# Down projection of a hybrid layer: the product P2 last, its resident blocks loaded ahead, the final norm by half rows

## The chip, the cores and the metric

The kernel runs on one core of one Trainium2 chip. The metric is the device time of that core in microseconds; smaller is better. Three runs of the kernel before took 1548.82, 1553.07 and 1555.38 us, so the median is 1553.07 us. One more execution was taken with the hardware profiler; all rows below come from it.

## What is computed

The kernel is one layer of a diffusion backbone: an adaLN-modulated norm, a token mixer with a gated DeltaNet and a Mamba-2 part, an output projection with a gated residual, then a gated MLP with a 3x3 convolution and a second gated residual, and a final RMSNorm. The change touches only what follows the MLP's gate, the down projection and the final norm. Of the reference:

```python
D_MODEL = 1024; SEQ = 1024; D_FF = 2816; EPS = 1e-6

def conv_glu(h, w_gate, w_up, conv_w, conv_b, w_down, on_grid):
    a = h @ w_gate
    ...
    return (jax.nn.silu(a) * (h @ w_up)) @ w_down

def rmsnorm(x, g):
    x32 = x.astype(jnp.float32)
    y = x32 * lax.rsqrt(jnp.mean(x32 * x32, axis=-1, keepdims=True) + EPS)
    return (y * g.astype(jnp.float32)).astype(x.dtype)

        x = x + g2 * conv_glu(modulate(rmsnorm(x, norm2_g[l]), sh2, sc2), *ffn_params, True)
    ...
    return rmsnorm(x, final_norm_g)
```

## The kernel before, in words

The down projection multiplies a 1024 x 2816 matrix by a 2816 x 1024 one. Both are cut into 2 x 2 parts and seven products P1 to P7 replace the usual eight (Strassen's method in Winograd's form): sums of parts go into a product, and sums of products give the four quarters of the result. The four quarters are tokens 0 to 511 or 512 to 1023 (row tiles t = 0 to 3 or 4 to 7 of 128 tokens each) by columns 0 to 511 (`LOH`) or 512 to 1023 (`HIH`). While the gate and up products run, `asums` and `wsums` write the sums of parts to DRAM (`sa_d`, `sw_d`).

Each product is a sum over 11 blocks (`NP`). `block` (L1407 and after) loads two tiles of 128 x 512 floats, 256 KB each, on the SP queue (L1418): `ra` from `sa_d`, the stationary side, and `rb` from `sw_d` or from `w_down`, the moving side. Each tile is split into a high part, a rounded copy that ACT makes (L1419, `sh` and `vh`), and a low part, a subtraction on DVE (recorded at the helper's line L95, `sl` and `vl`). `mul` (L1433) then makes three matmuls for each of four row tiles, so 12 in a block: high by high, and the two mixed ones. There are two buffers each for `ra` and `rb`, three each for `sh`, `sl`, `vh`, `vl`.

The eight PSUM banks form two sets of four, `accA` and `accB`. Products alternate between them, so a product's banks are read out ("evacuated") while the next product runs in the other set. The order is P1, P6, P2, P7, P5, P4, P3. The evacuation after each product keeps sums in `s1`, `s2`, `s3` (`sn` in the rows, 128 x 512 for each row tile) and, once a quarter is whole, `put` multiplies it by the gate row `g2row` into a temporary `tm` and adds that to the residual `x1[t]` (`x` in the rows): two DVE operations of 128 x 512.

The last product, P3, is treated apart. Its first three blocks (`HEAD`) run as the others do. For its last eight, the high and low parts go to eight places of their own in `mxh` and `mxl`, tiles that held the MLP's input before and are free by then; these are called resident blocks here. Then, for each row tile t, all matmuls of the eight resident blocks are to follow, then `put` and `final`.

`final(t, last)` is the norm of a whole row tile: ACT squares 128 x 1024 values and sums them along the row, DVE adds the epsilon, POOL raises the sum to the power -1/2 (L1289), DVE multiplies the row tile by that and by the gain row `gfrow` (one SCALAR_TENSOR_TENSOR, L107), and two DMAs write the halves, one from the SP queue and one from ACT's (L1573). For the last row tile it goes by halves (power at L1569). `final` runs for tiles 4 to 7 after P4, so beside P3, and for tiles 0 to 3 at the end.

The order on each engine is made when the kernel is built: a scheduler of the language places the instructions by its own estimate of their times, and each engine then runs its list strictly in order. A late instruction holds up all behind it on its engine.

Of the kernel before, what the change touches and what calls it, by code (L numbers as in the profile page):

```python
# [13 lines left out]
ALU = mybir.AluOpType  # L14
# [59 lines left out]
def hybrid_layer(ctx: ExitStack, tc: tile.TileContext, x, c, cx, c_ctx, w_ada, b_ada, norm1_g, w_in,  # L74
# [1325 lines left out]
    PRODS = ("P1", "P6", "P2", "P7", "P5", "P4", "P3")  # L1400
# [34 lines left out]
    def product(p, acc, js, first, last):  # L1435
        for j in js:
            ops = block(p, j, *parts())
            for t in range(4):
                mul(acc[t], t, ops, first and j == js[0], last and j == js[-1])

# [96 lines left out]
    with pool("p3") as p3:  # L1537
# [15 lines left out]
        def final(t, last):  # L1553
            if "f" not in rows:
                rows["f"] = T(p3, [P, D], "gfrow")
                nc.sync.dma_start(rows["f"], final_norm_g.partition_broadcast(P))
            jk = T(p3, [P, D], f"fj{t}", tag="fj", bufs=2)
            ot = T(p3, [P, D], f"ot{t}", tag="ot", bufs=3)
            halves = [slice(0, 512), slice(512, D)]
            if not last:  # L1560
                rs = rstd_tok(x1[t], jk, t, 1)
                stt(ot, x1[t], rs, rows["f"], ALU.mult, ALU.mult)
            else:
                rs, a = ss2[:, 1, t:t + 1], ss2[:, 0, 0:2]
                for c, q in enumerate(halves):
                    act(jk[:, q], x1[t][:, q], AF.Square, accum_out=a[:, c:c + 1])
                tt(rs, a[:, 0:1], a[:, 1:2], ALU.add)
                ts(rs, rs, 1.0 / D, ALU.mult, EPS, ALU.add)
                nc.gpsimd.tensor_tensor(rs, rs, mhalf[:, 0:1], op=ALU.pow)  # L1569
            for c, q in enumerate(halves):  # L1570
                if last:
                    stt(ot[:, q], x1[t][:, q], rs, rows["f"][:, q], ALU.mult, ALU.mult)
                (nc.scalar if c else nc.sync).dma_start(out[t * P:(t + 1) * P, q], ot[:, q])  # L1573

        allj = range(NP)
        product("P6", accB, range(NP - 1), True, False)
# [6 lines left out]
        product("P2", accA, allj, True, True)  # L1583
        for t in range(4):
            m = tmp_()
            tt(m, accA[t], s1[:, t, :], ALU.add)
            put(t, LOH, m)
        product("P7", accB, allj, True, True)
        for t in range(4):
            tt(s3[:, t, :], accB[t], s2[:, t, :], ALU.add)  # L1590
# [57 lines left out]
```

## Time and profile before

| what | value |
|---|---|
| median of three runs | 1553.07 us (1548.82 to 1555.38) |
| the profiled execution's own time | 1557.59 us |
| its span (first to last event of the core) | 1555.9 us |
| TensorE (PE) busy | 1454.9 us, 94% |
| VectorE (DVE) busy | 1093.4 us, 70% |
| ScalarE (ACT) busy | 695.1 us, 45% |
| GpSimd (POOL) busy | 514.8 us, 33% |
| matmuls of the seven products (L1433), part of the chain that ended last | 13% of the span |

The rows below are from the profiled execution, with times counted from the start of its span. The profiled time is 1.7 us longer than its span. "Idle before" in brackets is how long an engine stood still before an instruction, with what ended the wait. The granted clock (PEclk) is the share of TensorE's full clock that the chip allowed in a stretch.

### The profile page before, as it was taken

Reading aid. Unit: us, or ns where it says so; the run is one execution under the profiler, and the core shown is the slowest. Engines: PE = TensorE matmul, PEld = TensorE weight load, DVE = VectorE, ACT = ScalarE, POOL = GpSimd, SP = SyncE. Lnnn points to the kernel's source line nnn. Section 1 sums busy time; section 2 is a strip of 40 time slices with the busy share of each in tenths; the row PEclk is TensorE's granted clock in tenths of the full one; section 3 lists DMA queues with packets and bytes.
Section 4 is the critical chain, followed back from the end, with each engine's and each line's share of the span. In section 5 each row is a group of like instructions: output and inputs, shape, how many; then the busy total and the mean of one; then the engine's idle time right before and its main releaser. Section 6 shows DMA issues by size and latency. Waiting matters only on the chain.

```text
span 1555.9 us, 23948 instructions
## 1 busy us (share of the span) xinstructions
PE 1454.9 (94%) x8344; PEld 1213.3 (78%) x8344; DVE 1093.4 (70%) x1749; ACT 695.1 (45%) x1552; POOL 514.8 (33%) x645
## 2 busy tenths in 40 slices
PE   6899888899998889999988899999999999999996
PEld 2477766787888789998767688888888888888885
DVE  5877678887535676546977787777778777456597
ACT  6566555645676556545243432222222221344444
POOL 3554389793225784301373111011111111000002
PEclk8999999989999999999999999999999999999998
DMA  8344777745659686444952434344444433566655
GB/s 280 115 146 133 238 208 206 189 144 124 179 163 301 204 271 186 128 139 138 311 181 68 149 104 143 126 149 155 142 156 142 156 120 122 177 190 193 199 184 196
DMA packets 255415, 266.72 MB, mean 171 GB/s; under 512 B 50656, under 2 KB 193629, under 8 KB 255295
## 3 DMA queue, kind: packets, MB, share of 16 engines
q1 hardware_dynamic: 238815, 212.90, 45.2%
q0 software_dynamic: 15136, 49.55, 8.6%
q10 hardware_dynamic: 1344, 2.75, 0.5%
q8 instruction: 66, 1.08, 0.3%
q14 instruction: 54, 0.44, 0.1%
HBM read 191.87 MB, written 73.27 MB: 170 GB/s over the span
## 4 chain that ended last, share of the span: by engine, by line
PE 70%; DVE 8%; DMA 8%; POOL 7%; issue 4%; ACT 2%; SPq 1%; POOLq 0%; DVEq 0%; ACTq 0%
PE bk L1298 31%; PE bk L1433 13%; PE bk L453 7%; PE bk L619 6%; POOL Zs L98 2%; POOL pr L98 2%; DMA rb<-rows_d 1%; PE bk L1346 1%; DMA R<-rows_d 1%; DMA awa<-in_w_ada_dram 1%; PE bk L997 1%; DMA rec<-sg_d 1%; PE bk L1005 1%; POOL rb L823 1%; DVE owl L95 1%
## 5 line engine op out<-in xcount | busy, mean ns | idle before, releaser
L1298 PE MATMUL bk<-mxh,fh 128*128 128x512 f32 x672 | 262.6, 391 | 5.2 <-DVE fac L95 5.2
L1298 PE MATMUL bk<-mxl,fh 128*128 128x512 f32 x672 | 262.6, 391 | 0.0
L1298 PE MATMUL bk<-mxh,fl 128*128 128x512 f32 x672 | 261.9, 390 | 0.0
L107 DVE SCALAR_TENSOR_TENSOR fac<-gpad,v,fac 128x1024 f32<-128x1024 f32 x176 | 225.0, 1281 | 9.8 <-ACT fac L92 6.9
L1298 PEld LDWEIGHTS bk<-mxh,fh 128*128 128x128 f32 x672 | 126.9, 189 | 31.9 <-DVE fac L95 5.6
L1298 PEld LDWEIGHTS bk<-mxh,fl 128*128 128x128 f32 x672 | 126.9, 189 | 26.6
L1455 ACT CAST fh<-fr 128x1024 fp32r<-128x1024 f32 x42 | 44.3, 1055 | 231.2 <-PE bk L1298 223.2
L1298 PEld LDWEIGHTS bk<-mxl,fh 128*128 128x128 f32 x672 | 126.9, 189 | 26.4
L1519 POOL DMA_DIRECT2D sa_d<-fac x44 | 23.8, 541 | 353.5 <-issue 214.6
L453 PE MATMUL bk<-hh,wh 128*128 128x512 f32 x320 | 129.5, 405 | 0.7 <-DVE v L254 0.7
L453 PE MATMUL bk<-hh,wl 128*128 128x512 f32 x320 | 129.6, 405 | 0.0
L453 PE MATMUL bk<-hl,wh 128*128 128x512 f32 x320 | 128.5, 402 | 0.0
L95 DVE TENSOR_TENSOR fl<-fr,fh 128x1024 fp32r<-128x1024 f32 x42 | 51.3, 1222 | 93.2 <-ACT fh L1455 93.2
L1433 PE MATMUL bk<-vl,sh 128*128 128x512 f32 x276 | 107.4, 389 | 0.0
L1433 PE MATMUL bk<-vh,sl 128*128 128x512 f32 x276 | 107.4, 389 | 0.0
L1419 ACT CAST sh<-ra 128x512 fp32r<-128x512 f32 x69 | 43.0, 624 | 116.5 <-PE bk L1433 99.1
L95 DVE TENSOR_TENSOR sl<-ra,sh 128x512 fp32r<-128x512 f32 x69 | 47.6, 689 | 61.8 <-ACT sh L1419 61.8
L1289 POOL TENSOR_TENSOR ss<-ss,mhalf 128x1 f32<-128x1 f32 x15 | 15.2, 1012 | 221.7 <-DVE ss L104 221.7
L1433 PE MATMUL bk<-vh,sh 128*128 128x512 f32 x276 | 75.7, 389 | 0.0
L453 PEld LDWEIGHTS bk<-hh,wh 128*128 128x128 f32 x320 | 61.7, 193 | 13.3 <-PE bk L252 0.9
L453 PEld LDWEIGHTS bk<-hh,wl 128*128 128x128 f32 x320 | 61.6, 193 | 13.0 <-issue 0.9
L453 PEld LDWEIGHTS bk<-hl,wh 128*128 128x128 f32 x320 | 61.5, 192 | 11.9 <-issue 0.2
(386 smaller groups left out, 3726.6 us busy)
## 6 DMA issues: line engine op xcount, KB each, us to landing
ra<-sa_d SPq DMA_DIRECT2D x77, 256.0 KB
kv<-kv_d SPq DMA_DIRECT2D x80, 192.0 KB
yq<-yq_d SPq DMA_DIRECT2D x64, 192.0 KB
awa<-in_w_ada_dram SPq DMA_DIRECT2D x24, 512.0 KB
fr<-in_ffn_w_up_dram SPq DMA_DIRECT2D x22, 512.0 KB
dr<-in_ffn_w_down_dram SPq DMA_DIRECT2D x22, 512.0 KB
sa_d<-fac POOLq DMA_DIRECT2D x44, 256.0 KB, 2.3
rb<-sw_d SPq DMA_DIRECT2D x44, 256.0 KB
```

Source lines behind the costliest of these rows:

```text
L95: nc.vector.tensor_tensor(o, a, b, op=op)
L98: nc.gpsimd.tensor_tensor(o, a, b, op=op)
L107: nc.vector.scalar_tensor_tensor(o, a, s, b, op0=op0, op1=op1)
L453: paced(nc.tensor.matmul(pb[:, :bn], w[i][:, kk, :], hview(h, k, b0, bn), start=(n == 0), stop=(n == 3 * KT - 1)))
L619: mm = nc.tensor.matmul(pb[:, 256 * j:256 * j + 256], m[:, k, tk], w, start=(n == 0), stop=(n == 3 * KT - 1))
L823: nc.gpsimd.affine_select(e, e, pattern=[[0, n], [sg, P]], compare_op=ALU.is_ge, fill=-BIG, base=0, channel_multiplier=-sg)
L997: mm = nc.tensor.matmul(hi[d], yq[:, 0, :], r, start=True, stop=True)
L1298: nc.tensor.matmul(pv, w(k), h[:, b4, k, :], start=(n == 0), stop=(n == 3 * KT - 1))
L1419: nc.scalar.copy(th, raw)
L1433: nc.tensor.matmul(pb, a[:, tk], w, start=start and n == 0, stop=stop and n == 2)
L1455: hi["last"] = nc.scalar.copy(wh, raw)
L1519: nc.gpsimd.dma_start(sa_d[i][j], t)
```

## The change

The order of the products becomes P1, P6, P7, P5, P4, P3, P2, so the last one is P2. Its eight resident blocks are loaded and split during the five products in front of it: two during P6, two during P7, two during P5, one each during P4 and P3 (`ahead`; the numbers are the blocks after which one is placed). The final norm works on halves of rows. `half1` takes the first finished half of a row tile: it squares and sums it, adds the epsilon, and multiplies the half by the gain row in place. `half2` takes the other half: it squares and sums it, adds both sums, takes the power on POOL, multiplies this half by power and gain on DVE, and the first half by the power on ACT (`AF.Copy` with a scale), both in place, and writes both. The gain row is multiplied by 32 once on ACT, in place of the division by 1024. The columns of tiles 0 to 3 that come from P2 no longer go through `tm`; their two terms are put separately.

```diff
--- before.py
+++ after.py
@@ -1397,7 +1397,7 @@
     accA = accB = None
 
 
-    PRODS = ("P1", "P6", "P2", "P7", "P5", "P4", "P3")
+    PRODS = ("P1", "P6", "P7", "P5", "P4", "P3", "P2")
     STA = dict(P1=0, P2=1, P4=2, P3=3, P5=4, P6=5, P7=6)
     MOV = dict(P5=0, P6=1, P7=2, P4=3)
     WD = dict(P1=(0, 0), P2=(1, 0), P3=(1, 1))
@@ -1432,11 +1432,13 @@
         for n, (a, w) in enumerate(((sh, vh), (sh, vl), (sl, vh))):
             nc.tensor.matmul(pb, a[:, tk], w, start=start and n == 0, stop=stop and n == 2)
 
-    def product(p, acc, js, first, last):
+    def product(p, acc, js, first, last, between=None):
         for j in js:
             ops = block(p, j, *parts())
             for t in range(4):
                 mul(acc[t], t, ops, first and j == js[0], last and j == js[-1])
+            if between is not None:
+                between(j)
 
     with pool("fp") as fp:
         for n_, b_ in (("wr", 3), ("wh", 3), ("wl", 3)):
@@ -1550,68 +1552,84 @@
             tt(x1[t][:, q], x1[t][:, q], m, ALU.add)
 
 
-        def final(t, last):
-            if "f" not in rows:
-                rows["f"] = T(p3, [P, D], "gfrow")
-                nc.sync.dma_start(rows["f"], final_norm_g.partition_broadcast(P))
-            jk = T(p3, [P, D], f"fj{t}", tag="fj", bufs=2)
-            ot = T(p3, [P, D], f"ot{t}", tag="ot", bufs=3)
-            halves = [slice(0, 512), slice(512, D)]
-            if not last:
-                rs = rstd_tok(x1[t], jk, t, 1)
-                stt(ot, x1[t], rs, rows["f"], ALU.mult, ALU.mult)
-            else:
-                rs, a = ss2[:, 1, t:t + 1], ss2[:, 0, 0:2]
-                for c, q in enumerate(halves):
-                    act(jk[:, q], x1[t][:, q], AF.Square, accum_out=a[:, c:c + 1])
-                tt(rs, a[:, 0:1], a[:, 1:2], ALU.add)
-                ts(rs, rs, 1.0 / D, ALU.mult, EPS, ALU.add)
-                nc.gpsimd.tensor_tensor(rs, rs, mhalf[:, 0:1], op=ALU.pow)
-            for c, q in enumerate(halves):
-                if last:
-                    stt(ot[:, q], x1[t][:, q], rs, rows["f"][:, q], ALU.mult, ALU.mult)
-                (nc.scalar if c else nc.sync).dma_start(out[t * P:(t + 1) * P, q], ot[:, q])
+        gf = rows["f"] = T(p3, [P, D], "gfrow")
+        nc.sync.dma_start(gf, final_norm_g.partition_broadcast(P))
+        nc.scalar.mul(gf, gf, float(D) ** 0.5)
+        sq = T(p3, [P, 2, NLC], "sq")
+
+        def square(t, c, q):
+            cnt[0] += 1
+            jk = T(p3, [P, 512], f"fj{cnt[0]}", tag="fj", bufs=2)
+            act(jk, x1[t][:, q], AF.Square, accum_out=sq[:, c, t:t + 1])
+
+        def half1(t, q, c):
+
+            square(t, 0, q)
+            ts(sq[:, 0, t:t + 1], sq[:, 0, t:t + 1], D * EPS, ALU.add)
+            tt(x1[t][:, q], x1[t][:, q], gf[:, q], ALU.mult)
+
+        def half2(t, q, c):
+            square(t, 1, q)
+            rs = ss2[:, 1, t:t + 1]
+            tt(rs, sq[:, 0, t:t + 1], sq[:, 1, t:t + 1], ALU.add)
+            nc.gpsimd.tensor_tensor(rs, rs, mhalf[:, 0:1], op=ALU.pow)
+            o = HIH if q is LOH else LOH
+            stt(x1[t][:, q], x1[t][:, q], rs, gf[:, q], ALU.mult, ALU.mult)
+            act(x1[t][:, o], x1[t][:, o], AF.Copy, scale=rs)
+            nc.sync.dma_start(out[t * P:(t + 1) * P, q], x1[t][:, q])
+            nc.scalar.dma_start(out[t * P:(t + 1) * P, o], x1[t][:, o])
+
+
+        HEAD = NP - NLC
+        rest = []
+
+        def ahead(at):
+            def f(j):
+                if j in at:
+                    u = len(rest)
+                    sta, mov = ([m[:, u, 4 * i:4 * i + 4, :].rearrange("p k c -> p (k c)") for m in mxs]
+                                for i in range(2))
+                    rest.append(block("P2", HEAD + u, sta, mov))
+            return f
 
         allj = range(NP)
-        product("P6", accB, range(NP - 1), True, False)
+        product("P6", accB, range(NP - 1), True, False, ahead((3, 8)))
         product("P1", accA, [NP - 1], False, True)
         for t in range(4):
             nc.scalar.copy(s1[:, t, :], accA[t])
         product("P6", accB, [NP - 1], False, True)
         for t in range(4):
             tt(s2[:, t, :], accB[t], s1[:, t, :], ALU.add)
-        product("P2", accA, allj, True, True)
+        product("P7", accA, allj, True, True, ahead((3, 8)))
+        for t in range(4):
+            tt(s3[:, t, :], accA[t], s2[:, t, :], ALU.add)
+        for t in range(4):
+            put(t, LOH, s1[:, t, :])
+        product("P5", accB, allj, True, True, ahead((4, 9)))
         for t in range(4):
             m = tmp_()
-            tt(m, accA[t], s1[:, t, :], ALU.add)
-            put(t, LOH, m)
-        product("P7", accB, allj, True, True)
+            tt(m, accB[t], s3[:, t, :], ALU.add)
+            tt(s2[:, t, :], accB[t], s2[:, t, :], ALU.add)
+            put(4 + t, HIH, m)
+            half1(4 + t, HIH, 1)
+        product("P4", accA, allj, True, True, ahead((6,)))
         for t in range(4):
-            tt(s3[:, t, :], accB[t], s2[:, t, :], ALU.add)
-        product("P5", accA, allj, True, True)
+            put(t, HIH, s2[:, t, :])
         for t in range(4):
             m = tmp_()
-            tt(m, accA[t], s3[:, t, :], ALU.add)
-            tt(s2[:, t, :], accA[t], s2[:, t, :], ALU.add)
-            put(4 + t, HIH, m)
-            put(t, HIH, s2[:, t, :])
-        product("P4", accB, allj, True, True)
+            tt(m, s3[:, t, :], accA[t], ALU.subtract)
+            put(4 + t, LOH, m)
+            half2(4 + t, LOH, 0)
+        product("P3", accB, allj, True, True, ahead((4,)))
+        product("P2", accA, range(HEAD), True, False)
         for t in range(4):
-            m = tmp_()
-            tt(m, s3[:, t, :], accB[t], ALU.subtract)
-            put(4 + t, LOH, m)
-            final(4 + t, False)
-        HEAD = NP - NLC
-        product("P3", accA, range(HEAD), True, False)
-        ops = []
-        for u in range(NLC):
-            sta, mov = ([m[:, u, 4 * i:4 * i + 4, :].rearrange("p k c -> p (k c)") for m in mxs] for i in range(2))
-            ops.append(block("P3", HEAD + u, sta, mov))
+            put(t, HIH, accB[t])
+            half1(t, HIH, 1)
         for t in range(4):
             for u in range(NLC):
-                mul(accA[t], t, ops[u], False, u == NLC - 1)
-            put(t, HIH, accA[t])
-            final(t, t == 3)
+                mul(accA[t], t, rest[u], False, u == NLC - 1)
+            put(t, LOH, accA[t])
+            half2(t, LOH, 0)
 
     for name, ap in dbg.items():
         src = dict(rows=rows_d, xs=sg_d[0][:, :, 0:2, :], kv0=kv_d[0][:, :, 0:3, :], zs=zs_d)[name]
```

What the scheduler made of it is seen at three places. In the lists, `128x512` is the output's shape; numbers behind names are buffers.

**DVE, during P4.** The block of P4 with index 7 (its low parts are `sl894`, `vl894` before and `sl871`, `vl871` now) and what stands in front of it. `tm` and `x1` rows belong to evacuations, `sq` rows are sums of squares, `mxl` rows are the low parts of a resident block. Before:

```order
L95 TENSOR_TENSOR sl891_14333<-ra892_14336,sh891_14332 128x512
L95 TENSOR_TENSOR tm869_14176<-sn1_13034,g2row_9621 128x512
L95 TENSOR_TENSOR vl891_14335<-rb893_14340,vh891_14334 128x512
L95 TENSOR_TENSOR x1_6_8733<-x1_6_8733,tm868_14173 128x512
L95 TENSOR_TENSOR tm870_14179<-bk683_12788,sn2_13035 128x512
L95 TENSOR_TENSOR sn1_13034<-bk683_12788,sn1_13034 128x512
L95 TENSOR_TENSOR x1_2_8729<-x1_2_8729,tm869_14176 128x512
L95 TENSOR_TENSOR sl894_14357<-ra895_14360,sh894_14356 128x512
L95 TENSOR_TENSOR vl894_14359<-rb896_14364,vh894_14358 128x512
```

Now:

```order
L95 TENSOR_TENSOR mxl_8506<-ra869_14140,mxh_8505 128x512
L95 TENSOR_TENSOR tm884_14247<-sn1_13034,g2row_9621 128x512
L102 TENSOR_SCALAR sq_13043<-sq_13043 128x1
L95 TENSOR_TENSOR x1_6_8733<-x1_6_8733,gfrow_13040 128x512
L95 TENSOR_TENSOR mxl_8506<-rb870_14144,mxh_8505 128x512
L95 TENSOR_TENSOR x1_0_8727<-x1_0_8727,tm883_14244 128x512
L95 TENSOR_TENSOR tm885_14250<-sn1_13034,g2row_9621 128x512
L102 TENSOR_SCALAR sq_13043<-sq_13043 128x1
L95 TENSOR_TENSOR x1_7_8734<-x1_7_8734,gfrow_13040 128x512
L95 TENSOR_TENSOR x1_1_8728<-x1_1_8728,tm884_14247 128x512
L95 TENSOR_TENSOR sl871_14149<-ra872_14152,sh871_14148 128x512
L95 TENSOR_TENSOR vl871_14151<-rb873_14156,vh871_14150 128x512
```

Between P5's first evacuation and the end of `vl` of that block, both included, there were 32 operations of 128 x 512; now there are 39, and four of 128 x 1. Of the 39, twelve stand behind `vl` of P4's block 6: eight of evacuations and gain multiplications (the first two of them ahead of the rows shown), two of the resident block, and the two of block 7 itself.

**PE, at the end of the program.** The last matmuls; `bk_12785` to `bk_12788` are the banks of row tiles 0 to 3. Before:

```order
L1433 MATMUL bk_12785<-mxh 128x512
L1433 MATMUL bk_12786<-mxh 128x512
L1433 MATMUL bk_12787<-mxh 128x512
L1433 MATMUL bk_12788<-mxh 128x512
L1433 MATMUL bk_12785<-mxl,mxh 128x512
L1433 MATMUL bk_12785<-mxh,mxl 128x512
L1433 MATMUL bk_12786<-mxl,mxh 128x512
L1433 MATMUL bk_12786<-mxh,mxl 128x512
```

Now:

```order
L1433 MATMUL bk_12787<-mxh 128x512
L1433 MATMUL bk_12787<-mxl,mxh 128x512
L1433 MATMUL bk_12787<-mxh,mxl 128x512
L1433 MATMUL bk_12788<-mxh 128x512
L1433 MATMUL bk_12788<-mxl,mxh 128x512
L1433 MATMUL bk_12788<-mxh,mxl 128x512
```

Before, every resident block was multiplied for all four row tiles before the next block, so all four banks ended with the last block. Now all 24 matmuls of a row tile stand together, and the four banks end one after the other.

**ACT, during the last product but one.** `fj` rows are squares with their sums, `x1` rows the scaling of the first half by the power `ss2`. Before, in P3 with its resident blocks:

```order
L1419 CAST mxh_8505<-ra923_14578 128x512
L1419 CAST mxh_8505<-rb924_14582 128x512
L92 ACTIVATE fj4_14459,ss2_138<-x1_4_8731 128x1024
L1419 CAST mxh_8505<-ra925_14586 128x512
L1419 CAST mxh_8505<-rb926_14590 128x512
L1419 CAST mxh_8505<-ra927_14594 128x512
L92 ACTIVATE fj5_14472,ss2_138<-x1_5_8732 128x1024
L1419 CAST mxh_8505<-rb928_14598 128x512
```

Now, in P3 as an ordinary product:

```order
L92 ACTIVATE x1_4_8731<-x1_4_8731,ss2_138 128x512
L1419 CAST sh911_14404<-ra912_14408 128x512
L1419 CAST vh911_14406<-rb913_14412 128x512
L92 ACTIVATE fj892_14274,sq_13043<-x1_5_8732 128x512
L1580 DMA out_0_dram<-x1_4_8731 128x512
L1419 CAST mxh_8505<-ra914_14428 128x512
L1419 CAST mxh_8505<-rb915_14432 128x512
L92 ACTIVATE fj895_14287,sq_13043<-x1_6_8733 128x512
L92 ACTIVATE x1_5_8732<-x1_5_8732,ss2_138 128x512
L1419 CAST sh916_14436<-ra917_14440 128x512
L1419 CAST vh916_14438<-rb918_14444 128x512
```

Now the casts `sh911` and `sh916`, which P3's blocks 4 and 5 need, stand behind a scaling that waits for the power of its row tile.

## Rows read from the trace of the kernel before

**Rows 1.** The page: span, part 1 (engines), and of part 2 the granted clock.

```profile
span 1555.9 us, 23948 instructions
...
PE 1454.9 (94%) x8344; PEld 1213.3 (78%) x8344; DVE 1093.4 (70%) x1749; ACT 695.1 (45%) x1552; POOL 514.8 (33%) x645
...
PEclk8999999989999999999999999999999999999998
```

**Rows 2.** Chain that ended last, in order of time: start us, us, what.

```profile
1333.42 207.41 PE bk L1433 x915
```

**Rows 3.** Timeline, 1539.5 to 1556: start us, us, engine line op out<-in xcount [idle].

```profile
1540.43 0.39 PE L1433 MATMUL bk<-mxh,mxl 128*128 128x512 f32 x1
...
1540.85 1.29 DVE L95 TENSOR_TENSOR tm<-bk,g2row 128x512 f32<-128x512 f32 x2 [2.01 <-PE bk L1433]
...
1541.79 0.39 PE L1433 MATMUL bk<-mxh,mxl 128*128 128x512 f32 x1
1542.06 0.68 DVE L95 TENSOR_TENSOR x<-x,tm 128x512 f32<-128x512 f32 x1
...
1542.83 1.06 ACT L92 ACTIVATE fj<-x 128x1024 f32<-128x1024 f32 x1 [4.71 <-DVE x L95]
...
1546.29 0.61 ACT L92 ACTIVATE fj<-x 128x512 f32<-128x512 f32 x1
...
1546.81 0.19 ACT L92 ACTIVATION_READ_ACCUMULATOR fj<-x 128x1 f32 x1
...
1550.42 0.14 DVE L104 TENSOR_SCALAR ss<-ss 128x1 f32<-128x1 f32 x1
1550.65 0.55 POOL L1569 TENSOR_TENSOR ss<-ss,mhalf 128x1 f32<-128x1 f32 x1 [1.46 <-DVE ss L104]
1551.23 1.41 DVE L107 SCALAR_TENSOR_TENSOR ot<-x,ss,gfrow 128x512 f32<-128x512 f32 x2 [0.66 <-POOL ss L1569]
```

**Rows 4.** Timeline: ACT, DVE and SP queue around two loads of blocks.

```profile
1381.51 0.62 ACT L1419 CAST sh<-ra 128x512 fp32r<-128x512 f32 x1 [1.58 <-PE bk L1433]
...
1382.16 0.69 DVE L95 TENSOR_TENSOR sl<-ra,sh 128x512 fp32r<-128x512 f32 x1 [1.42 <-ACT sh L1419]
...
1382.88 0.32 SPq L1418 DMA_DIRECT2D ra<-sa_d  x1
...
1488.01 0.32 SPq L1418 DMA_DIRECT2D ra<-sa_d  x1
...
1490.75 0.62 ACT L1419 CAST sh<-ra 128x512 fp32r<-128x512 f32 x1 [2.02 <-DMA ra<-sa_d]
```

**Rows 5.** Timeline: P5's first evacuation, P4's first matmuls, one P4 block.

```profile
1481.29 0.69 DVE L95 TENSOR_TENSOR tm<-bk,sn 128x512 f32<-128x512 f32 x1
...
1482.17 1.07 PE L1433 MATMUL bk<-vh,sh 128*128 128x512 f32 x4
...
1499.92 0.68 DVE L95 TENSOR_TENSOR vl<-rb,vh 128x512 fp32r<-128x512 f32 x1
```

**Rows 6.** Timeline: the power on POOL beside running DVE operations.

```profile
1518.27 2.75 POOL L1289 TENSOR_TENSOR ss<-ss,mhalf 128x1 f32<-128x1 f32 x1 [180.63 <-DVE ss L104]
...
1519.91 0.68 DVE L95 TENSOR_TENSOR mxl<-rb,mxh 128x512 fp32r<-128x512 f32 x1
...
1521.05 1.28 DVE L107 SCALAR_TENSOR_TENSOR ot<-x,ss,gfrow 128x1024 f32<-128x1024 f32 x1 [0.46 <-POOL ss L1289]
```

**Rows 7.** Timeline of PE: two matmuls that followed a stop.

```profile
811.70 0.72 PE L1346 MATMUL bk<-owl,mxh 128*128 128x512 f32 x1 [2.25 <-DVE owl L95]
...
894.36 0.79 PE L1298 MATMUL bk<-mxh,fh 128*128 128x512 f32 x1 [5.18 <-DVE fac L95]
```

**Rows 8.** Busy time by stretch, behind those stops: engines (x instructions), PEclk, DMA, GB/s.

```profile
812.00:815.00 3.00, 3.00 (x8) 2.32 (x8) 3.00 (x3) 3.00 (x7) 3.00 (x2) 0.50 0.31 104
815.00:818.00 3.00, 3.00 (x17) 2.43 (x17) 2.39 (x4) 1.76 (x4) 1.11 (x3) 0.96 0.21 65
894.36:902.00 7.64, 7.64 (x21) 6.04 (x22) 7.13 (x7) 3.21 (x5) 0.54 (x1) 0.59 0.22 71
```

## The prediction

> **What bounds the kernel now.** I read four things, in this order. First the page [rows 1]: PE is busy 94% of the span and its clock is at full speed nearly everywhere in the second half. Then the chain that ended last [rows 2]: from 1333.42 us on, 207.41 us of it are the seven products' matmuls without a gap, at 207.41 / 915 = 0.227 us each, so 2.72 us for a block of 12. In this stretch only PE counts; ACT, DVE and the loads are ahead of it. Third, the timeline of the end [rows 3]: the last matmul starts at 1541.79 and takes 0.39, so PE is done at 1542.18, and the span ends at 1555.9. These last 13.7 us are evacuation, norm and output of four row tiles one after the other, with PE idle. Fourth, the reserve that ACT, DVE and the loads have over PE, which decides what a moved piece of work costs [rows 4, 5].
>
> **What the change can gain: the end.** The number of matmuls is the same, so PE's own work is unchanged. But all four banks used to end together, and now a row tile has 24 x 0.227 = 5.4 us of PE to itself; tiles 0 to 2 are normed and written beside the matmuls of the next. Behind the last matmul stands tile 3 alone, and of it half a row. Its chain, from [rows 3]: bank to DVE 0.03 (1540.82 to 1540.85); two DVE operations, 0.60 for the first, since they start 0.60 apart, and 0.68 for the second; DVE to ACT 0.09; square of a half, 0.52 until its sum is read, and 0.19 for reading; ACT to DVE 0.10, an estimate next to the other handoffs; adding the sums 0.14; DVE to POOL 0.09; the power 0.55; 0.03; multiplying a half 0.70 (1.41 for two; ACT's scaling of the other half, 0.61 like its square, runs beside it); and from there to the end of the span 3.26, as from 1552.64 to 1555.9 now, for issue and landing. The sum is 7.0 us in place of 13.7, a **gain of 6.7**. It is smallest, 4.5, if the power takes 2.75, the longest of these rows [rows 6].
>
> Of the power, the rows show two prices: 0.55 at the end, with DVE idle, and 2.75 at 1518.27, where it ended at 1521.02, 0.43 after the last of a run of DVE operations that read two SBUF tensors (1519.91 + 0.68) [rows 3, 6]. The Trainium skill (SBUF — State Buffer, Who interferes with whom) says that a VectorE instruction with two SBUF inputs contends with a GpSimd one that reads SBUF, and that the loser blocks. The trace agrees. With the free price everywhere, the 1.2 us found for P3 below would be 0 and the whole sum 1.2 lower.
>
> **What it costs: the loads.** Eight resident blocks move to where PE is full. Each adds two DMAs of 256 KB, two casts and two subtractions in front of a block that PE will need; their total number is unchanged. Each buffer `ra` or `rb` goes round in 2.74 (issue to cast, when the load alone ends the wait), 0.65 to the subtraction and 0.72 to the next issue, 4.11 in all [rows 4]; with two buffers a block can come every 2.06, and PE takes one every 2.72. So 13 blocks in one product need 26.8 of its 29.9 us. The reserve: a cast starts when the block three earlier leaves its buffer, the last low part is there 1.95 later (0.65 + 0.60 + 0.69), and PE wants it after two more blocks and four matmuls, 6.35: 4.4 us to spare. A resident block alone takes 2.06 of these. Nothing is lost where DVE has no other work, and I cost the loads in P7, P5 and P3 at nothing for that reason; without this cover each costs its 2.06.
>
> **Where DVE has other work.** Before, the evacuations of P5 are 24 operations beside P4. Now 20 of the evacuation and gain, 8 of the `put` for tiles 0 to 3 and 2 of the resident block stand there. In order on one engine, what counts is how many precede a block's last low part. Before, that of P4's block 7 is the 32nd from P5's first evacuation: 1499.92 against 1481.29, so 18.63 / 31 = 0.601 each [rows 5]. P4 starts 0.88 behind that first evacuation; PE wants block 7's low part at 0.88 + 7 x 2.72 + 0.91 = 20.8, and it is ready at 19.3. Now it is the 39th with four tiny ones (0.06 each) in front: 38 x 0.601 + 0.24 + 0.68 + 0.03 = 23.8. PE stops for **3.0 us**. The bounds are 0, if part of this is done earlier than I count, and 4.
>
> In P7, eight operations of the early `put` add 4.8 against the reserve of 4.4: **0.4** (0 to 1). In P3, ACT scales tile 5 ahead of the casts of block 5. DVE has 21 operations and two tiny ones until it needs that power, 12.7, with the first power's wait and a cast's some 13.2; the power ends 0.43 later, then scaling 0.61 and two casts of 0.6, so 15.4; PE wants the casts at 1.3 + 5 x 2.72 = 14.9. That is 0.5, and the next tile does the same with a square (0.7) in between: **1.2** in all (0 to 2.5). In P2 the 12 operations of the last evacuation lie beside 8.2 us of HEAD and 5.4 of tile 0, and no low part waits behind them. The gain row's multiplication by 32 (1.06 on ACT, as a 128 x 1024 square) and the other added ACT work lie where ACT idles 1.58 a block [rows 4], at nothing; without that cover it would be 1.06. Its DMA keeps its place on SP.
>
> **The clock.** A stop of 3.0 us can cost more than itself. Behind a stop of 2.25, PE's granted clock was 0.50 over 3 us and 0.96 over the next 3; behind one of 5.18 it was 0.59 on the mean of 7.64 us [rows 7, 8]. Half is 1.2 in place of 2.4 GHz. What is lost is the length times the missing share: 1.5 + 0.1 = 1.6, and 3.1. A stop of 3.0 is nearer to 2.25, so I take **1.7**, with 0 and 3.1 as ends. What speaks against it: PE has been full for over 150 us before this stop [rows 2, 5].
>
> **The sum.** -6.7 + 3.0 + 0.4 + 1.2 + 1.7 = -0.4 us. The profiled execution took 1557.59, so it would be 1557.2; it stands 4.5 over the median of the runs, 1553.07. Against that median I predict **1552.7 us**.
>
> **The rivals.**
> - *The stops come, the clock stays*: -6.7 + 4.6 = -2.1, so 1551.0. For it: the 150 full us before the stop. Against it: neither stop of [rows 7] kept its clock.
> - *No stop*: the order's reserve holds everywhere and only the end counts: -6.7, so 1546.4. For it: PE had no stop at all in 207 us, with DVE full for much of P4 [rows 5]. Against it: the count of 39, by the method that gives the 32nd right.
> - *Slower than before*: the stops in P4 and P3 both bring the clock down, at 3.1 and 1.7: -2.1 + 4.8 = +2.7, so 1555.8; with a power of 2.75 at the end as well, 1558.0. It decides as soon as stops and clock together pass 6.7. For it: the same DVE list holds back P4 and then, through POOL and ACT, P3. Against it: while PE runs at half speed DVE catches up, and the P3 stops are short.
>
> **How the numbers follow.** Chances: the forecast 0.40, clock stays 0.23, no stop 0.22, slower 0.15. All lie close. The range reaches from 1546.0, just past the no-stop case, to 1557.0, between the two times of the slower rival. What a measurement of this kernel can tell from no change is about 0.5%, 7.8 us, so faster means below 1545.3: the end alone gives 6.7, and only a shorter landing (two last DMAs in place of four close together) or a larger gain takes it there: 0.11. Slower means above 1560.8, 7.7 of net loss: 0.05. The rest, 0.84, is no difference that can be told.
>
> **What would show it.** Right: the last matmul some 7 us from the span's end, with one row tile's chain behind it; PE stops of about 3 us on a DVE low part two thirds through P4, and shorter ones on ACT casts in P3; a granted clock under 1 behind the first. Wrong: no PE stops in the seven products (then the time is near 1546), an end that still takes over 10 us, stops behind the resident loads in P6 or P5, or a time outside the range.

## The result, and the profile after

The changed kernel takes 1559.3 us (median of 8 runs, 1555.8 to 1561.2). Runs of the kernel before on the same chip have a median of 1552.0. The ratio is 1.0048, with a 95% interval of 1.0034 to 1.0062, so it is 7 us slower. The forecast was 1552.7, no difference that can be told, with a range of 1546 to 1557; the measured time lies outside it. The profiled execution took 1559.39, close to the median.

The page of the changed kernel, against [rows 1]:

```profile
span 1557.7 us, 23978 instructions
...
PE 1459.2 (94%) x8344; PEld 1214.7 (78%) x8344; DVE 1100.3 (71%) x1767; ACT 706.8 (45%) x1575; POOL 514.5 (33%) x645
...
PEclk8999999999999999999999999999999999999999
```

Its busy times say little. The chain that ended last does (start us, us, what); of [rows 2]'s 207 us without a gap, these are the pieces of the seven products:

```profile
1330.45 39.91 PE bk L1433 x176
...
1401.23 63.23 PE bk L1433 x276
...
1475.65 9.85 PE bk L1433 x35
...
1501.56 4.64 DMA ra<-sa_d
1508.67 35.73 PE bk L1433 x156
```

The chain leaves PE after 1370.36, 1464.46 and 1485.50 and comes back for good at 1508.67; between the pieces it runs through DVE, ACT, POOL and loads. From the first matmul of the unbroken run to the last end it is 1330.29 to 1549.83, 219.5 us, against 1333.25 to 1542.18, 208.9: **10.6 us lost in the products**.

The end, as a timeline of the last row tile, against [rows 3]:

```profile
1549.44 0.39 PE L1433 MATMUL bk<-mxh,mxl 128*128 128x512 f32 x1
1549.87 0.69 DVE L95 TENSOR_TENSOR tm<-bk,g2row 128x512 f32<-128x512 f32 x1 [1.66 <-PE bk L1433]
1550.60 0.69 DVE L95 TENSOR_TENSOR x<-x,tm 128x512 f32<-128x512 f32 x1
1551.32 0.63 ACT L92 ACTIVATE fj<-x 128x512 f32<-128x512 f32 x1 [3.14 <-DVE x L95]
...
1552.32 0.55 POOL L1575 TENSOR_TENSOR ss<-ss,mhalf 128x1 f32<-128x1 f32 x1 [4.89 <-DVE ss L95]
...
1552.90 0.75 DVE L107 SCALAR_TENSOR_TENSOR x<-x,ss,gfrow 128x512 f32<-128x512 f32 x1 [0.66 <-POOL ss L1575]
```

Matmuls end at 1549.83 and the span at 1557.7: 7.8 us in place of 13.7, so **5.9 gained**. Net that is +4.7 in this pair of profiles. A second profile of each gave 13.3 lost, 5.9 gained, net +7.4; the medians of the runs stand 7.3 apart.

What changed is who lets ACT cast. Summed waits from 1325 us on (engine line, waited for: us in total, times, longest), before:

```profile
ACT sh L1419 <- PE bk L1433: 99.1, 55, 19.4
...
ACT sh L1419 <- DMA ra<-sa_d: 9.5, 5, 2.7
```

and after:

```profile
ACT sh L1419 <- PE bk L1433: 38.1, 17, 19.4
ACT sh L1419 <- DMA ra<-sa_d: 34.4, 31, 3.1
```

Before, 55 casts waited for PE to hand a buffer back, and so were early. After, 17 do, and 31 wait for a load: most of the lead, the time by which loads and casts run ahead of PE, is gone. In P5, timeline of ACT and SP, against [rows 4]:

```profile
1424.99 0.62 ACT L1419 CAST sh<-ra 128x512 fp32r<-128x512 f32 x1
...
1431.39 0.32 SPq L1418 DMA_DIRECT2D ra<-sa_d  x1
...
1434.87 0.62 ACT L1419 CAST sh<-ra 128x512 fp32r<-128x512 f32 x1 [1.12 <-DMA ra<-sa_d]
...
1451.96 0.62 ACT L1419 CAST sh<-ra 128x512 fp32r<-128x512 f32 x1 [0.77 <-DVE vl L95]
```

From 1424.99 to 1451.96 there are 12 turns of `ra` (from one cast out of it to the next), so 2.25 us each, not 2.06. A load ends the wait in 8 of the 12, DVE in 3, PE in 1. The casts that waited for their load start 2.65 to 3.48 behind its issue, 3.0 on the mean, not 2.74; the longest is the one issued at 1431.39. At [rows 4] mostly one pair of loads was under way, here two. So P5's 13 blocks need 29.25 of its 29.92 us, and hardly anything of a used lead comes back. P4 starts like this (timeline, PE, ACT, DVE), against [rows 5]:

```profile
1450.57 0.62 ACT L1419 CAST vh<-rb 128x512 fp32r<-128x512 f32 x1 [0.65 <-DMA rb<-sw_d]
...
1450.65 1.07 PE L1433 MATMUL bk<-vh,sh 128*128 128x512 f32 x4
...
1451.22 0.69 DVE L95 TENSOR_TENSOR vl<-rb,vh 128x512 fp32r<-128x512 f32 x1 [0.58 <-ACT vh L1419]
1451.83 0.68 DVE L95 TENSOR_TENSOR tm<-bk,sn 128x512 f32<-128x512 f32 x1
```

The first evacuation, `tm` at 1451.83, starts 1.18 behind P4's first matmul; before it was 0.88 ahead. It stands in DVE's list behind the low part `vl` of block 1, and that came late. From there on the count of the prediction holds: block 7's `vl` ends 23.8 behind 1451.83 (1474.92 + 0.68). PE's stops in P7, P4 and P3, against [rows 7]:

```profile
1401.23 1.20 PE L1433 MATMUL bk<-vh,sh 128*128 128x512 f32 x4 [0.74 <-ACT vh L1419]
...
1471.80 1.21 PE L1433 MATMUL bk<-vh,sh 128*128 128x512 f32 x4 [1.07 <-ACT vh L1419]
...
1474.92 0.68 DVE L95 TENSOR_TENSOR vl<-rb,vh 128x512 fp32r<-128x512 f32 x1
...
1475.65 0.50 PE L1433 MATMUL bk<-vl,sh 128*128 128x512 f32 x1 [2.64 <-DVE vl L95]
...
1508.67 1.21 PE L1433 MATMUL bk<-vh,sh 128*128 128x512 f32 x4 [1.15 <-ACT vh L1419]
```

The granted clock behind the longest (windows; PEclk is the third number from the end), against [rows 8]:

```profile
1475.00:1477.00 2.00, 1.35 (x5) 1.07 (x6) 2.00 (x4) 0.32 (x1) 0.00 (x0) 0.84 0.45 120
1477.00:1479.00 2.00, 2.00 (x6) 1.59 (x5) 2.00 (x4) 1.24 (x2) 0.00 (x0) 0.50 0.75 267
1479.00:1481.00 2.00, 2.00 (x8) 1.60 (x7) 1.38 (x3) 0.62 (x1) 0.00 (x0) 0.80 0.63 174
```

What is missing there, window length times missing share, is 2 x (0.16 + 0.50 + 0.20) = 1.7 us.

### The profile page after: what moved, and what is told of

It reads as the page before. It is cut to its first block, busy times and chain, and to the rows that moved or that the text cites. A ratio compares the mean times of both kernels' runs of the same rounds, so it can differ in the third digit from the quotient of the medians.

```text
span 1557.7 us, 23978 instructions
## 1 busy us (share of the span) xinstructions
PE 1459.2 (94%) x8344; PEld 1214.7 (78%) x8344; DVE 1100.3 (71%) x1767; ACT 706.8 (45%) x1575; POOL 514.5 (33%) x645
## 3 DMA queue, kind: packets, MB, share of 16 engines
q10 hardware_dynamic: 1344, 2.75, 0.5%
## 4 chain that ended last, share of the span: by engine, by line
PE 65%; DMA 11%; DVE 9%; POOL 5%; issue 5%; ACT 3%; SPq 1%; POOLq 0%; ACTq 0%; DVEq 0%
PE bk L1298 31%; PE bk L1433 10%; PE bk L453 8%; PE bk L619 5%; DMA R<-rows_d 2%; DMA rb<-rows_d 2%; PE bk L1346 1%; POOL Zs L98 1%; POOL pr L98 1%; DVE owl L95 1%; DMA ra<-sa_d 1%; DMA owr<-in_w_out_dram 1%; PE bk L997 1%; PE bk L533 1%; DMA u_d<-rb 1%
## 5 line engine op out<-in xcount | busy, mean ns | idle before, releaser
L1575 POOL TENSOR_TENSOR ss<-ss,mhalf 128x1 f32<-128x1 f32 x8 | 8.6, 1069 | 209.6 <-DVE ss L95 209.6
```

## The experiments

All twelve runs are in one table. A product's loss is the time from its first matmul to the next product's, less the 29.92 that it takes in the kernel before; it holds stops and slow clock. "End" is from the last matmul's end to the span's end, "sum" is the losses and the end together. The ratio is to the kernel before, from the runs, with its 95% interval.

| kernel | P1, P6 | P7 | P5 | P4 | P3 | P2 | end | sum | ratio |
|---|---|---|---|---|---|---|---|---|---|
| before | 0 | 0 | 0 | 0 | 0 | 0 | 13.7 | 13.7 | 1 |
| before_again | 0 | 0 | 0 | 0 | 0 | 0 | 13.7 | 13.7 | one run |
| changed | 0 | 1.3 | 0.1 | 6.8 | 2.5 | 0 | 7.8 | 18.4 | 1.0048 (1.0034 to 1.0062) |
| after_again | 0 | 1.3 | 0.8 | 8.6 | 2.5 | 0 | 7.8 | 21.1 | 1.0047 (1.0028 to 1.0066) |
| x1_noahead | 0 | 0 | 0 | 1.2 | 1.3 | 2.1 | 9.8 | 14.5 | 0.9993 (0.9977 to 1.0008) |
| x2_put | 0 | 0.9 | 0 | 3.0 | 3.5 | 0 | 7.8 | 15.2 | 1.0033 (1.0017 to 1.0050) |
| x3_spread | 0 | 0.3 | 3.4 | 2.7 | 0.6 | 0 | 7.8 | 15.0 | 1.0029 (1.0014 to 1.0043) |
| x6_rows | 0 | 0.7 | 0 | 4.4 | 2.8 | 0.2 | 7.8 | 16.0 | 1.0036 (1.0022 to 1.0050) |
| y2_p5one | 0 | 3.6 | 0.7 | 7.8 | 2.5 | 0 | 7.8 | 22.4 | 1.0032 (1.0015 to 1.0050) |
| y1_five | 0 | 0 | 0 | 0 | 1.2 | 1.0 | 8.4 | 10.6 | 0.9976 (0.9960 to 0.9992) |
| z6_slow | 2.5 | 3.7 | 0 | 0.4 | 1.2 | 0 | 7.8 | 15.7 | 1.0022 (1.0005 to 1.0039) |
| z7_slow_put | 1.3 | 4.4 | 0 | 0 | 0 | 0 | 7.8 | 13.5 | 1.0014 (0.9995 to 1.0033) |
| z5_five_slow | 1.4 | 2.0 | 0 | 0 | 0 | 1.0 | 8.4 | 12.8 | 0.9994 (0.9976 to 1.0012) |
| w1_late_put | 2.5 | 2.5 | 1.8 | 0 | 1.7 | 0 | 7.8 | 16.4 | 0.9989 (0.9971 to 1.0006) |

A sum is one execution, a ratio the middle of many; the two differ by up to 4.4 us. The intervals of x2, x3, x6, y2 and z6 overlap with the changed kernel's, so their gains over it (1.9 to 4.0 us by the ratios) are not clear of noise; what is read from them below is read from one trace each. Those of x1, y1, z5, z7 and w1 lie below its 1.0034 to 1.0062.

**x1_noahead**: no block ahead; the residents are loaded behind P2's first three blocks.

```diff
-        product("P4", accA, allj, True, True, ahead((6,)))
+        product("P4", accA, allj, True, True)
...
         product("P2", accA, range(HEAD), True, False)
+        late_ = ahead(range(NLC))
+        for u in range(NLC):
+            late_(u)
```

> Order of the products, norm by halves and evacuations as changed, but the eight resident blocks of P2 are loaded behind its first three blocks, as the kernel before did. Theory (stops add up: what the evacuation and the norm put on DVE meets a reserve that the resident loads ahead have used): without the loads ahead block 7's last low part in P4 is the 33rd DVE operation (39th in the changed kernel) and the loads have their turns back, so P4 stops for 0 to 0.3 us in place of 5.0 and its clock stays full; P7 stops 0.3 in place of 1.3; P3 keeps most of its 2.4, since the scaling on ACT still waits there for the power. The end is the old one in length, since the four banks end together: some 10 to 12 us behind the last matmul. Time some 3 us below the changed kernel, 1554 to 1558. Rival (the resident loads alone make all the stops): no stop in P7, P4 and P3. Second rival (the time is lost in another stretch than the seven products): stops gone and time still near 1559 or above.

P7 and P5 lose nothing, P4 1.2 where at most 0.3 was expected. The time, 1552.0, is the kernel before's and lies below the 1554 to 1558 that was expected. So neither theory nor rival is whole: the loads ahead make most of the loss in P4, but the evacuation and norm still make 1.2 there, all of it behind block 7, and 1.3 in P3 without them.

**x2_put**: eight operations out of P4, four into P3's evacuation.

```diff
-        for t in range(4):
-            put(t, HIH, s2[:, t, :])
...
-            put(t, HIH, accB[t])
+            m = tmp_()
+            tt(m, accB[t], s2[:, t, :], ALU.add)
+            put(t, HIH, m)
```

> Only the eight DVE operations that add P4's contribution to tiles 0 to 3 (columns 512 to 1023) are taken out of P4 and joined with P3's in its evacuation, four sums in place of eight put operations. Block 7's last low part in P4 is then the 34th DVE operation in place of the 39th. Theory: the stop at that block falls by 5 x 0.60 = 3.0 us, from 5.0 in P4 as a whole to 2.0; the clock behind it may keep its level (1.7 back). So 3.0 to 4.7 us below the changed kernel: 1554.6 to 1556.3. P7 (1.3) and P3 (2.4) keep their stops. Rival (the resident loads and their turns make the stops, DVE's list doesn't matter): P4 stops for 5 us as before, time as the changed kernel, 1559.

P4 loses 3.0 in place of 6.8 and its clock stays at 1.00: DVE's list does matter. By the ratios it is 2.3 us below the changed kernel, less than the 3.0 to 4.7 expected. P3 loses 1.0 more, most of its loss in one stop (timeline, ACT and PE, with the window behind it):

```profile
1494.45 0.72 ACT L92 ACTIVATE x<-x,ss 128x512 f32<-128x512 f32 x1 [1.56 <-POOL ss L1575]
...
1496.25 1.20 PE L1433 MATMUL bk<-vh,sh 128*128 128x512 f32 x4 [2.47 <-ACT vh L1419]
...
1496.00:1499.00 3.00, 2.75 (x12) 2.24 (x13) 2.91 (x6) 2.47 (x6) 0.79 (x2) 1.00 0.91 306
```

Here is the stop that the prediction saw for P3: ACT's scaling waits 1.56 for a power on POOL, with a cast behind it.

**x3_spread**: the places alone: P6 (0, 3, 6), P7 (5, 8), P5 (2, 4, 6), none in P4 and P3.

```diff
-        product("P5", accB, allj, True, True, ahead((4, 9)))
+        product("P5", accB, allj, True, True, ahead((2, 4, 6)))
```

> Only the places of the resident loads change: three during P6, two late in P7, three in the front half of P5, none in P4 and P3. DVE's other work stays where the change put it. Block 7's last low part in P4 is the 33rd DVE operation, and the loads have seven blocks of P5 to win back their turns before P4. Theory: P4's stop 0 to 0.3 in place of 5.0 and its clock stays full (1.7), P3 keeps 1 to 2.4, P7 0.4 to 1.3; P5 may stop by up to 1 where three residents stand within five blocks. So some 6 to 7.5 us below the changed kernel, 1552 to 1553.5. Rival (each resident block costs its 2.06 us wherever it stands): the stops move to P5 and P6 and the time stays within 2 us of the changed kernel.

Expected 1552 to 1553.5, measured 1556.8. The rival came closer: stops of 3.4 move into P5, though none into P6. Timeline, SP, ACT and PE:

```profile
1426.67 0.32 SPq L1418 DMA_DIRECT2D ra<-sa_d  x1
...
1427.88 0.32 SPq L1418 DMA_DIRECT2D ra<-sa_d  x1
...
1430.64 1.21 PE L1433 MATMUL bk<-vh,sh 128*128 128x512 f32 x4 [0.85 <-ACT vh L1419]
...
1431.90 0.62 ACT L1419 CAST sh<-ra 128x512 fp32r<-128x512 f32 x1 [1.31 <-DMA ra<-sa_d]
...
1437.53 1.20 PE L1433 MATMUL bk<-vh,sh 128*128 128x512 f32 x4 [1.12 <-ACT vh L1419]
```

Of two pairs issued 1.2 apart the second is cast late: 1427.88 to 1431.90 is 4.0 where 2.74 was counted. And P4, with no resident load of its own, still loses 2.7, 1.1 of it up to block 7: its first evacuation starts 0.86 behind P4's first matmul.

**x6_rows**: tiles 4 to 7 normed by whole rows on DVE.

```diff
-            stt(x1[t][:, q], x1[t][:, q], rs, gf[:, q], ALU.mult, ALU.mult)
-            act(x1[t][:, o], x1[t][:, o], AF.Copy, scale=rs)
+            if t < 4:
+                stt(x1[t][:, q], x1[t][:, q], rs, gf[:, q], ALU.mult, ALU.mult)
+                act(x1[t][:, o], x1[t][:, o], AF.Copy, scale=rs)
+            else:
+                stt(x1[t], x1[t], rs, gf, ALU.mult, ALU.mult)
```

(`half1` multiplies by the gain for t < 4 only.)

> Tiles 4 to 7 are normed by whole rows again: no gain multiplication of the first half in P4, no scaling on ACT in P3, one 128 x 1024 multiplication on DVE in place of both. Tiles 0 to 3 keep the halves. Theory: P3's stops come from ACT's scaling waiting for a power on POOL ahead of casts; without it they fall from 2.4 to under 0.5. In P4 block 7's last low part is the 35th DVE operation in place of the 39th, so the stop falls by 4 x 0.60 = 2.4, to some 2.6, with the clock as it may be (0 to 1.7 back). Together 4 to 6.5 us below the changed kernel, 1553 to 1555.5. Rival (P3's stops come from its resident load or the output DMAs on the SP queue): P3 keeps some 2 us and the gain is 2.4 or less.

By the ratios it is 1.9 us below the changed kernel; 4 to 6.5 was expected. P4 came as counted, 2.4 less. P3 did not: it loses 2.8, without any scaling on ACT. Those are the rival's numbers (P3 keeps some 2, the gain is 2.4 or less). The wait seen here is one of DVE for the power, in front of low parts (timeline, DVE and PE):

```profile
1496.43 1.29 DVE L107 SCALAR_TENSOR_TENSOR x<-x,ss,gfrow 128x1024 f32<-128x1024 f32 x1 [0.44 <-POOL ss L1576]
...
1499.65 0.50 PE L1433 MATMUL bk<-vl,sh 128*128 128x512 f32 x1 [1.44 <-DVE vl L95]
```

So ACT's scaling cannot be all of P3's cause. The rival names two causes. P3's resident load is absent in x3, which still loses 0.6 there, and in x1, which loses 1.3. The outputs stand in every run. The changed kernel's trace has rows for them: its chain runs in P3 through a load that takes 4.64 us, with outputs of row tiles issued while it is under way (timeline, SP and ACT):

```profile
1501.56 0.32 SPq L1418 DMA_DIRECT2D ra<-sa_d  x1
...
1503.33 0.37 ACTq L1580 DMA_DIRECT2D out_dram<-x  x1
1503.35 0.34 SPq L1579 DMA_DIRECT2D out_dram<-x  x1
...
1506.27 0.62 ACT L1419 CAST sh<-ra 128x512 fp32r<-128x512 f32 x1 [1.85 <-DMA ra<-sa_d]
```

The cast starts 4.71 behind the issue, and the next load's 4.94. No run takes the outputs away, so how much of P3's loss they make is open.

**y2_p5one**: the block behind P5's block 9 goes into P6.

```diff
-        product("P6", accB, range(NP - 1), True, False, ahead((3, 8)))
+        product("P6", accB, range(NP - 1), True, False, ahead((0, 3, 6)))
-        product("P5", accB, allj, True, True, ahead((4, 9)))
+        product("P5", accB, allj, True, True, ahead((4,)))
```

> The changed kernel with one resident block moved: the one behind P5's block 9 goes into P6, which then takes three; one each in P4 and P3 as changed. Theory (that block cost one turn of the loads just ahead of P4, so that P4's evacuation started 1.18 us behind P4's first matmul in place of 0.88 ahead of it, and that is the difference between 3.0 and 5.0 us): the evacuation starts some 0.9 ahead of P4 again, the stops in P4 come to 3.0 and the clock's fall to 0 to 1.7; P7 and P3 as changed. So 2 to 3.7 us below the changed kernel, 1555.5 to 1557.5. Rival (the length of DVE's list alone sets P4's stops, whatever came before): 5 us and the same time as the changed kernel.

Missed: P4 lost 7.8, and its evacuation began 1.11 behind. It was not the one block close to P4. With three resident blocks in P6, P7 lost 3.6 in place of 1.3: the lead was spent earlier. P5 has 12 blocks here, yet from 1433.26 to 1456.50 its ten turns of `ra` take 2.32 each, so a block wins back 0.40 of lead, where the prediction had 2.72 - 2.06 = 0.66.

**after_again** and **before_again**: both kernels once more.

> The changed kernel once more, for its spread. Theory: stops in the same places, 9 to 11.5 us in all with the clock's part, the end 7.9, and a median of 1559. Rival (the stops differ by several us from execution to execution): another profile of the same kernel shows stops that differ by over 2 us in P4 or P3.

> The kernel before once more, for the spread of what lies ahead of the products: P7 began at 1392.41 us in its first profile, with a time near the top of its runs. Theory: no stop in the products, the end 13.7, and the start of the products earlier by about what the time is lower. Rival: stops or a different end in this execution.

The kernel before repeats to 0.05 us from the first matmul of the products on. (The product that begins at 1392.41 in its first profile is P2; P7 begins at 1422.33.) In the changed kernel P4's first evacuation was 1.82 behind this time, its stops 5.7 and the clock's part 2.9. The places are the same, the sizes differ by 2.7: 13.3 us in the products, over the 9 to 11.5 expected, with P4 1.8 apart.

**z6_slow**, **z7_slow_put** (z6 with the edit of x2), **z5_five_slow** (z7 with five residents): residents through one buffer of their own.

```diff
-            raw = T(p2, [P, 512], f"{'rb' if which else 'ra'}{cnt[0]}", tag="rb" if which else "ra", bufs=2)
+            if p == "P2" and j >= own_[0]:
+                raw = T(own_[1], [P, 512], f"rc{cnt[0]}", tag="rc", bufs=1)
+            else:
+                raw = T(p2, [P, 512], f"{'rb' if which else 'ra'}{cnt[0]}", tag="rb" if which else "ra", bufs=2)
```

(`own_` holds `HEAD` and the pool `p3`.)

> The changed kernel with one edit: the resident blocks are loaded through one buffer of their own (256 KB, taken in turn by both sides) in place of the two pairs that the products use. Casts, subtractions and traffic are the same; the order then has them from P1's last blocks to the middle of P7, none later. Theory (the price of a resident block is a turn of the products' load buffers, taken out of a reserve that P4's evacuation needs): no stops from P1 to P7 beyond 1 us, since the products' turns are their own; P4 stops 1 to 1.5 in place of 6.8 to 8.6, as without loads ahead, and its clock stays full; P3 1 to 2.5; the end 7.9. Stops and end 10 to 12 us against the 13.7 of the kernel before: 2 to 3.5 us faster than before, 8 to 10 below the changed kernel. Rival (it is the traffic, 512 KB a block, that slows the loads): stops of 5 us or more move into P6 and P7, and the time stays near 1558.

> As the run beside it (resident blocks through a buffer of their own), and P4's contribution to tiles 0 to 3 joins P3's, so that 20 operations in place of 28 stand beside P4. Theory: P4's remaining stop of 1 to 1.5 goes, P3 keeps 1 to 2; stops and end 9 to 10.5, 3 to 4.5 us faster than before. Rival (P3's evacuation in P2 takes the place of P4's): the stop comes back in P2 or P3 with over 2 us.

> Five resident blocks through a buffer of their own, and P4's contribution joined with P3's. Theory: stops at most 1 in P3 and 1 in P2 (its first six blocks run beside P3's evacuation), none before; the end 8.3; 10 in all, 3 to 4.5 us faster than before, like the kernel with five blocks in the common buffers. Rival (the joint buffers cost that kernel more in its untraced executions than its trace shows): 1 to 2 us faster than it.

In z6, P4 loses 0.4 with the changed kernel's whole evacuation beside it; in z7 and z5, with the joined put, it loses 0. P3, where ACT still scales behind POOL, loses 1.2, 0 and 0. In z7, P4 starts with its lead intact (timeline, DVE and PE):

```profile
1448.02 0.69 DVE L95 TENSOR_TENSOR tm<-bk,sn 128x512 f32<-128x512 f32 x1
...
1448.87 0.84 PE L1437 MATMUL bk<-vh,sh 128*128 128x512 f32 x3
```

0.85 ahead, as before. But the rival is half right: P1, P6 and P7, where the residents now stand, lose 3.4 to 6.2, and with that the times missed. Gains of 2 to 4.5 us were expected; z7 and z5 show none, and z6 is 0.2% slower than the kernel before. The largest stop is at P7's second block (z7, timeline, PE):

```profile
1390.89 0.50 PE L1437 MATMUL bk<-vl,sh 128*128 128x512 f32 x1 [2.25 <-DVE vl L95]
```

**w1_late_put**: z7, and the early `put` is held behind P7's evacuation.

```diff
+            tc.add_manual_dep(put(t, LOH, s1[:, t, :]).ins, e3.ins.name, NOSYNC, reason="put behind P7")
```

> As the kernel with resident blocks through a buffer of their own and P4's contribution joined with P3's, and the early put (eight DVE operations for columns 0 to 511 of tiles 0 to 3) is held behind P7's evacuation, so that it stands in P5, where DVE has little else, and no longer in front of P7's second block. Theory: the stop of 3.3 us on that block's low part goes and P7 keeps under 1.5; P5 stops 0 to 1, P4, P3 and P2 0; the end 7.8. Stops and end 10 to 11 us against 13.7: 3 to 4 us faster than before. Rival (the stop in P7 comes from the resident load that stands there, not from the put): P7 keeps 3 us or more and the time stays near before.

P7's second block lost 0.5 in place of 3.3, so that stop did come from the put. But P7 as a whole, P5 and P3 still lose 2.5, 1.8 and 1.7, and the ratio is no different from 1: the 3 to 4 us expected did not come.

**y1_five**: five residents in place of eight, at P6 (0, 3, 6), P7 (8), P5 (5), with the edit of x2.

```diff
-        HEAD = NP - NLC
+        NRES = 5
+        HEAD = NP - NRES
...
-            for u in range(NLC):
-                mul(accA[t], t, rest[u], False, u == NLC - 1)
+            for u in range(NRES):
+                mul(accA[t], t, rest[u], False, u == NRES - 1)
```

> Five resident blocks in place of eight (the first six blocks of P2 run as the others do): three loaded during P6, one late in P7, one in the middle of P5, none in P4 and P3; and P4's contribution to tiles 0 to 3 joins P3's, as in the second of the first runs. So P4 and P3 have no load beyond their own, and DVE has 20 operations of evacuation beside P4 in place of 28. Theory (stops come where evacuation on DVE meets a reserve that resident loads have used): P4 stops 0 to 0.7 in place of 6.8 with its clock, P3 0 to 0.7 in place of 2.4, P7 0 to 1.3; the end stays near 7.9, since a row tile still has 15 matmuls, 3.4 us, to itself. Stops and end 8 to 10 us against the 13.7 us of the kernel before: 4 to 6 us faster than before, 1547 to 1549. Rival (something outside the five products costs some 3 us whenever blocks are loaded ahead, as the medians of the first four runs stand against their own traces): stops as above, time only 1 to 3 below before.

It beats both kernels: 1549.1 us, 3.7 us or 0.24% below the kernel before (the interval reaches from 0.08% to 0.40%; 4 to 6 us were expected), and 0.7% below the changed one (0.9976 / 1.0048). PE's waits from P7 on:

```profile
PE bk L1433 <- ACT vh L1419: 0.9, 1, 0.9
PE bk L1433 <- DVE vl L95: 0.6, 1, 0.6
```

The end is 5.3 shorter than before's, for 2.2 of losses in P3 and P2.

## Why the prediction was wrong

The sum said -0.4. In its terms the two profiles gave -5.9 for the end, 5.1 and 5.7 for P4's stops, 1.4 and 2.1 for P7 with P5, 2.5 for P3, 1.7 and 2.9 for the clock: with the rounding +4.7 and +7.4.

- **The failed step** is in "What it costs: the loads": the resident loads in P7, P5 and P3 at nothing, with a turn of 2.06 and 4.4 us to spare. The turn was worked out from a load with one pair under way. With both pairs under way it is 2.25 to 2.32, so a product of 13 blocks leaves 0.7 us, not 3.1, and the lead, once used, stays used. It runs out as early as P7, where PE stops, and again before P4.
- **What that did in P4.** The evacuation there starts 2.06 to 2.7 later against PE than counted, and P4's stop grows by just that: 1.18 + 23.8 - 19.95 = 5.0 in place of 3.0, where 19.95 is 7 x 2.72 + 0.91; measured 5.1. For the second profile the same gives 5.7; measured 5.7. With each kernel's own start and its own count of operations up to block 7's low part (39 in y2, 35 in x6, 34 in x2, 33 in x3, x1 and z6) the sum gives 5.0, 2.6, 2.8, 1.0 and, for x1 and z6, less than 0. PE's stops up to block 7 came to 5.0, 2.7, 3.0, 1.1, 0 and 0. So two things set this stop, where DVE's list starts and how long it is, and the prediction had the first wrong.
- **What shows that the loads made the late start** is the set of kernels. The evacuation starts ahead of P4 in before, x1, z6, z7, z5 and w1 (0.07 to 0.88), which lose 0 to 1.2 there. It starts 0.86 to 1.95 behind in the changed kernel, x2, x3, x6 and y2, which lose 2.7 to 8.6. Only y1 starts 0.30 behind and loses nothing, with 20 operations of evacuation in place of 28. In x1 only the loads ahead were taken away; the start is back at 0.88 ahead, and the count falls to 33 with them. z6 has all resident work and all 28 and loses 0.4; but its resident blocks also stand earlier, and its count is 33, so whether their own buffer or their place did it is not told apart.
- **The count on DVE** was right: the 39th operation, 23.8 us. Shorter lists gave smaller losses in P4, x2 by 3.8 with the clock's 1.7, and x6 by 2.4 with the clock as it was.
- **The clock**: 1.7 taken, with 3.1 as the upper end; 1.7 and 2.9 measured.
- **P7**: 0.4 forecast, 1.3 measured; the puts meet resident loads there, too. With the same puts and no loads ahead, x1 loses nothing in P7, and with one more resident block in P6, y2 loses 3.6.
- **P3**: 1.2 forecast, 2.5 measured. The mechanism, ACT's scaling behind a power of 2.13 to 2.75 ([rows 6]), is seen in x2, but P3 loses 1.2 in z6 and nothing in z7, where the loads have their lead. So it decides little by itself. The sum had no term for loads of 4.7 to 4.9 us beside the outputs. The kernel before has such a load in P3, too (issued at 1529.09, cast at 1533.79), and PE does not stop there; in z7 one of 4.6 costs nothing either.
- **The end**: 6.7 forecast, 5.9 measured. The second DVE operation starts 0.73 behind the first, not 0.60, and from the last multiplication's end to the span's end it is 4.0, not 3.26.
- Of the rivals, "slower than before" was nearest: stops and clock passed the end's gain, as it says. Its 1555.8 to 1558.0 was too low for the same reason, and P3's stops did not bring the clock down.

How P3's 2.5 is shared among the late start that P4 hands on, its own resident block and the outputs was not taken apart: no run has only one of the three removed.

## What to carry to other kernels

Price a turn of a load buffer in a stretch where all buffers are under way, not from one pair of loads, and add up all blocks of a stretch against its length: a lead that wins back nothing is spent once. An exposed end moved beside other work is paid from that lead, so move only as much as it covers. y1, with five of eight resident blocks, kept 5.3 of the end's 5.9 us and left the products nearly whole; it also changed their places and joined a put, and the three are not told apart. When two lists meet on an in-order engine, look where the first of them starts, not only at how long it is.

## What was not expected of the hardware

- With more loads under way a load takes longer from its issue to its cast: 2.74 us with one pair, up to 3.48 in P5 of the changed kernel, 4.0 in x3. The Trainium skill (DMA: Bandwidth & Descriptors, Latency and other measured facts) says that HBM's latency grows with load; these rows agree in direction, and no run shows that HBM is the place.
- A stop's length alone does not tell whether the clock falls. It fell to 0.50 behind 1.58 in x6, and to 0.66 on the mean of 3 us behind 2.25 in z7, but stayed at 1.00 behind 2.47 in x2 and behind 2.12 in P7 of z6. In x6 a stop of 0.62 stood 2.8 us ahead, in x2 PE had been full for the 3 us before; but in z6 one of 0.56 stood 6.3 us ahead, and z7, where one of 0.92 did, lost its clock. What decides is open.
- With the same order of instructions in front, the unbroken run of matmuls began anywhere from 1324.19 to 1333.25 in these profiles. Between the two profiles of the kernel before it is 5.5 us, all of the difference of their times. So sums here are taken from that point on.
